# Local attention on Trainium2: the weighted sum of the three dilations moved from VectorE to GpSimd for three heads out of four

## Chip, cores and metric

One core of a Trainium2 (trn2) chip runs the whole program in one launch. The metric is the time of the program on the device in microseconds (us), the median of several runs. A profiled execution lists what each engine did: TensorE (PE in the profile; its weight loads are PEld), VectorE (DVE), ScalarE (ACT), GpSimd (POOL) and SyncE (SP), which here issues the DMAs.

## The reference

A trunk of two decoder layers over 1024 positions of width 1024, all in float32. The first layer mixes with gated DeltaNet heads and short convolutions, the second (odd) layer with four HGRN2 heads and four heads of dilated local attention; a SwiGLU network follows each. The change lies in the second layer's local attention. Every head attends three times, with dilations 1, 4 and 16, and the three outputs are added with weights that come from their log-sum-exps:

```python
for p, (window, dilation) in enumerate(SWA_PATTERNS):      # (128, 1), (512, 4), (2048, 16)
    o_p, lse_p = dilated_window_attention(sq[:, :, p], sk[:, :, p], sv[:, :, p], window, dilation)
    outs.append(o_p)
    lses.append(lse_p)
wts = jax.nn.softmax(jnp.stack(lses, axis=-1), axis=-1)
o_d = jnp.einsum('bthpd,bthp->bthd', jnp.stack(outs, axis=3), wts).reshape(b, t, SWA_HEADS * SWA_DH)
return jnp.concatenate([o_c.astype(h.dtype), o_d.astype(h.dtype)], axis=-1) @ w_out
```

## The kernel before

Most of the program is projections on TensorE: a float32 operand is split into a high part (ScalarE, line 103) and a remainder (VectorE, line 104), and three matmuls of 128x512 (lines 136 to 138) give one product. Weights come by DMA into two buffers `raw`.

`mixer_cd` is the second layer's mixer. Its Python code is a set of generators: `hg_chain` steps through HGRN2's eight units (four heads by two halves of 512 positions), `loc` through attention, and `tick`, called between pieces of the projections, advances them, so that their small matmuls stand between large ones in the order of the program. Within this mixer the engines' own orders are not written out by hand: a planner orders each engine's instructions at build time from the program's order, the dependences and its own estimates of durations. The order is fixed in the finished program, each engine runs its list in order, and an instruction whose input is late holds up what stands behind it on that engine.

Attention runs dilation 4 first, then 16, then 1 (`p` is 1, 2, 0). The outputs of the first two go to DRAM (`scr_o`) with their maxima and sums in two more columns. When a half (`g`) of a head (`h`) is done for dilation 1, `output` copies it from PSUM to SBUF (`ol`, line 2456) and starts `combine(h, g, ol, sums)`, eight in all. A combine

- loads the other two outputs into `cm0` and `cm1` (line 2482, two buffers each, so that a load must wait until the combine before the last has done with them);
- works out the three weights `w3` in a string of tiny VectorE instructions of 128x4 (lines 2488 to 2499, the first two of which read `cm0` and `cm1`);
- scales `cm0` and `cm1` on ScalarE (line 2503, eight of 128x128);
- multiplies `ol` by its weight (line 2504) and adds `cm0` and `cm1` to it (line 2506, two), each 128x512 and each dependent on the one before;
- two steps of `loc` later transposes `ol` on TensorE (line 2511), copies the result out of PSUM (line 2513) and stores it for the output projection (line 2514).

Beside it the HGRN2 units use VectorE (lines 2153 to 2161: differences and products of 128x256; 2173 to 2287 others), ScalarE, and for a few instructions GpSimd: a copy (2160), four copies of 32x128 into `attn` (2214) and a power of 128x4 (`rr`, line 2264), which VectorE's line 2266 waits for.

Of the kernel before, what the change touches and what calls it, by code (L numbers as in the profile page):

```python
# [16 lines left out]
MULT, ADD, SUB, MAX, MIN = ALU.mult, ALU.add, ALU.subtract, ALU.max, ALU.min  # L17

P = 128
# [37 lines left out]
def hybrid_trunk_kernel(ctx: ExitStack, tc: tile.TileContext, x_t, w_all, w_down, w_ba, vecs, c_f, c_i, c_rope, out):  # L57
    nc = tc.nc
    V, S, G, T = nc.vector, nc.scalar, nc.gpsimd, nc.tensor
# [34 lines left out]
    def psu():  # L94
        return ps.tile([P, HT], F32, tag="u", name="psu", bufs=3)
# [2002 lines left out]
    def mixer_cd(hn, hp, qkd, wv):  # L2098
# [5 lines left out]
        with ExitStack() as es:  # L2104
            def tl(tag, shape=(HT,), bufs=1):
                return wp.tile([P] + list(shape), F32, tag=tag, name=tag, bufs=bufs)
# [245 lines left out]
            class Attend:  # L2352
# [90 lines left out]
                def output(self, n):  # L2443
# [15 lines left out]
                    if p == 0:  # L2459
                        late.append(combine(h, g, ol, sums))  # L2460
                        next(late[-1])
                        return
# [14 lines left out]
            def combine(h, g, ol, sums):  # L2477

                t, st = [ol], [sums]
                for p in range(2):  # L2480
                    a = tl(f"cm{p}", (4, 132), 2)
                    dma(a[:, :, 0:P + 2],
                        scr_o[h, p, g * HT:(g + 1) * HT].rearrange("(j i) d -> i j d", i=P)[:, :, 0:P + 2])
                    t.append(a)
                    st.append(a[:, :, P:P + 2])
                yield
                mx, dn, w3, tmp = tl("mx", (4,)), tl("dn", (4,)), tl("w3", (3, 4)), tl("tmp4", (4,))
                V.tensor_tensor(mx, st[0][:, :, 0], st[1][:, :, 0], op=MIN)
                V.tensor_tensor(mx, mx, st[2][:, :, 0], op=MIN)
                for p in range(3):  # L2490
                    V.tensor_tensor(w3[:, p, :], st[p][:, :, 0], mx, op=SUB)
                S.activation(w3, w3, AF.Exp, scale=-1.0)
                for p in range(3):
                    d = dn if p == 0 else tmp
                    V.tensor_tensor(d, w3[:, p, :], st[p][:, :, 1], op=MULT)
                    if p:
                        V.tensor_tensor(dn, dn, tmp, op=ADD)
                V.reciprocal(tmp, dn)
                V.tensor_tensor(w3, w3, tmp[:, None, :].to_broadcast([P, 3, 4]), op=MULT)
                for p in range(1, 3):  # L2500
                    for j in range(4):
                        x, w = t[p][:, j, 0:P], w3[:, p, j:j + 1]
                        S.activation(x, x, AF.Copy, scale=w)  # L2503
                V.tensor_tensor(ol[:, :, 0:P], ol[:, :, 0:P], w3[:, 0, :, None].to_broadcast([P, 4, P]), op=MULT)
                for p in range(1, 3):
                    V.tensor_tensor(ol[:, :, 0:P], ol[:, :, 0:P], t[p][:, :, 0:P], op=ADD)  # L2506
                yield
                yield
                o = psu()
                for j in range(4):  # L2510
                    T.transpose(o[:, j * P:(j + 1) * P], t[0][:, j, 0:P], ident)
                go = tl("sw", bufs=2)
                S.copy(go, o)
                dma(catd[g][4 + h], go)
# [133 lines left out]
    E = mybir.EngineType  # L2648
# [205 lines left out]
```

## Time and profile before

| | |
|---|---|
| median of 3 runs | 2501.08 us (2499.98 to 2502.36) |
| profiled execution | 2501.29 us, of which 2499.5 us are the profile's span |
| TensorE matmul busy | 2482.9 us, 99% of the span |
| TensorE weight load busy | 2057.6 us, 82% |
| VectorE busy | 1693.6 us, 68% |
| ScalarE busy | 1101.1 us, 44% |
| GpSimd busy | 626.9 us, 25% |
| granted TensorE clock | 0.999 |
| the first and the last start of a line-2504 instruction | 1689.1 and 1766.4 us |
| line 2504 on VectorE | 8 instructions, median 692 ns |
| line 2506 on VectorE | 16 instructions, median 692 ns |

Busy time is the time in which an engine had an instruction in work; an instruction that waits inside for a shared resource counts as busy. Matmuls overlap, so TensorE's busy share says that it hardly ever stood, not that it worked at its peak. Times in the text are counted from the start of the span.

### The profile page before, as it was taken

The page shows a single profiled execution, that of the slowest core. Times are in us where ns is not written, and L with a number is a line of the kernel's source. Part 1 is how long each engine was busy: PE and PEld are TensorE (multiplying, and loading weights), DVE is VectorE, ACT ScalarE, POOL GpSimd, SP SyncE. Part 2 cuts the span into 40 slices and gives each one's busy share as a digit, 9 for nine tenths or more (in the row PEclk, how much of TensorE's full clock was granted, in tenths as well). Part 3 has the DMA queues.
Part 4 walks back from the last instruction along what each step waited for, and adds up shares of the span by engine and source line. Part 5 has one row for each costly group of instructions (what it writes and reads, how often), then busy time and mean ns, then how long its engine had stood idle before and what let it go on. Part 6 is the DMA issues. An engine that isn't in the chain of part 4 may idle for free. (4 is left out here: it accounts for less than half of the span.)

```text
span 2499.5 us, 37191 instructions
## 1 busy us (share of the span) xinstructions
PE 2482.9 (99%) x13715; PEld 2057.6 (82%) x13715; DVE 1693.6 (68%) x2811; ACT 1101.1 (44%) x1932; POOL 626.9 (25%) x591
## 2 busy tenths in 40 slices
PE   9999999999999999999999999999999999999998
PEld 7888888888888888888888888888888888888887
DVE  8987775686656665567798647788667555656654
ACT  5432134343333345344677435567534333334442
POOL 1321111323333300031466401100132333330001
PEclk9999999999999999999999999999999999999999
DMA  4535458236566688643344467875833555658753
GB/s 157 165 122 166 136 167 270 102 109 208 195 207 217 204 291 297 191 138 138 130 154 139 150 213 250 209 213 185 280 108 113 169 185 188 218 201 294 275 177 126
DMA packets 292975, 466.16 MB, mean 187 GB/s; under 512 B 49944, under 2 KB 146744, under 8 KB 292536
## 3 DMA queue, kind: packets, MB, share of 16 engines
q1 hardware_dynamic: 292504, 463.26, 56.2%
q8 instruction: 108, 1.77, 0.3%
q10 hardware_dynamic: 288, 0.52, 0.1%
q14 instruction: 75, 0.61, 0.1%
HBM read 314.18 MB, written 149.50 MB: 186 GB/s over the span
## 5 line engine op out<-in xcount | busy, mean ns | idle before, releaser
L104 DVE TENSOR_TENSOR w<-raw,w 128x1024 fp32r<-128x1024 f32 (+1 forms) x333 | 394.3, 1187 | 147.3 <-ACT w L103 146.8
L103 ACT CAST w<-raw 128x1024 fp32r<-128x1024 f32 (+1 forms) x333 | 315.2, 954 | 283.9 <-PE psu L138 126.5
L136 PE MATMUL psu<-hnh,w 128*128 128x512 f32 x772 | 308.7, 400 | 0.0
L138 PE MATMUL psu<-hnh,w 128*128 128x512 f32 x772 | 301.3, 390 | 0.0
L137 PE MATMUL psu<-hnl,w 128*128 128x512 f32 x772 | 301.1, 390 | 0.0
L199 POOL TENSOR_TENSOR acc<-acc,sq 128x512 f32<-128x512 f32 x52 | 78.2, 1504 | 442.8 <-ACT sq L195 398.6
L338 POOL TENSOR_TENSOR ws<-raw 128x512 f32<-128x512 f32 x54 | 70.5, 1305 | 433.8 <-DMA raw<-in_dram 224.5
L136 PEld LDWEIGHTS psu<-hnh,w 128*128 128x128 f32 x772 | 145.0, 188 | 31.0 <-ACT sq L195 0.8
L138 PEld LDWEIGHTS psu<-hnh,w 128*128 128x128 f32 x772 | 144.9, 188 | 31.0
L137 PEld LDWEIGHTS psu<-hnl,w 128*128 128x128 f32 x772 | 145.2, 188 | 28.0
L104 DVE TENSOR_TENSOR w<-ws,w 128x1024 fp32r<-128x1024 f32 x51 | 70.8, 1388 | 105.3 <-ACT w L103 105.2
L104 DVE TENSOR_TENSOR hidq<-hr,hidq 128x1024 fp32r<-128x1024 f32 x72 | 82.3, 1145 | 77.3 <-ACT hidq L103 76.9
L103 ACT CAST hidq<-hr 128x1024 fp32r<-128x1024 f32 x72 | 70.2, 979 | 102.3 <-DMA hr<-ts 60.1
L429 POOL TENSOR_TENSOR hid<-hid,c 128x512 f32<-128x512 f32 x44 | 63.1, 1433 | 171.8 <-ACT hid L428 171.6
L136 PE MATMUL psm<-hidq,w 128*128 128x512 f32 (+1 forms) x275 | 106.1, 386 | 0.0
L137 PE MATMUL psm<-hidq,w 128*128 128x512 f32 (+1 forms) x275 | 105.8, 385 | 0.0
L138 PE MATMUL psm<-hidq,w 128*128 128x512 f32 (+1 forms) x275 | 105.8, 385 | 0.0
L136 PE MATMUL psu<-t3h,w 128*128 128x512 f32 x240 | 93.4, 389 | 0.0
L137 PE MATMUL psu<-t3l,w 128*128 128x512 f32 x240 | 93.4, 389 | 0.0
L138 PE MATMUL psu<-t3h,w 128*128 128x512 f32 x240 | 93.4, 389 | 0.0
L136 PE MATMUL psu<-t4h,w 128*128 128x512 f32 x240 | 93.4, 389 | 0.0
L137 PE MATMUL psu<-t4l,w 128*128 128x512 f32 x240 | 93.4, 389 | 0.0
(616 smaller groups left out, 6617.1 us busy)
## 6 DMA issues: line engine op xcount, KB each, us to landing
raw<-in_dram SPq DMA_DIRECT2D x229, 512.0 KB, 4.4
sd<-in_dram SPq DMA_DIRECT2D x44, 512.0 KB, 4.0
hid<-hid SPq DMA_DIRECT2D x88, 256.0 KB, 3.2
sd<-sd SPq DMA_DIRECT2D x44, 512.0 KB, 3.0
hr<-ts SPq DMA_DIRECT2D x40, 512.0 KB, 4.7
raw<-sd SPq DMA_DIRECT2D x40, 512.0 KB, 4.6
qk<-z SPq DMA_DIRECT2D x52, 256.0 KB, 4.1
hd<-h SPq DMA_DIRECT2D x48, 256.0 KB, 3.4
```

What stands on the lines that cost most here:

```text
L103: S.copy(hi, src)
L104: eng.tensor_tensor(lo, src, hi.bitcast(F32), op=SUB)
L136: T.matmul(o, lh, rh, start=first and i == 0, stop=False, **kw)
L137: T.matmul(o, lh, rl, start=False, stop=False, **kw)
L138: T.matmul(o, ll, rh, start=False, stop=last and i == n - 1, **kw)
L199: (eng or G).tensor_tensor(a, a, q, op=ADD)
L338: G.tensor_tensor(s[:, HT:], b[:, :HT], b[:, HT:], op=ADD)
L429: G.tensor_tensor(h, h, self.c22.pop(f), op=MULT)
```

## The change

For heads 0, 1 and 2 the multiplication and the two additions of a combine are issued on GpSimd (`G`), for head 3 they stay on VectorE (`V`). Operands, shapes, dependences and the order of the program stay as they were; 18 of the 24 instructions change engine.

```diff
                         x, w = t[p][:, j, 0:P], w3[:, p, j:j + 1]
                         S.activation(x, x, AF.Copy, scale=w)
-                V.tensor_tensor(ol[:, :, 0:P], ol[:, :, 0:P], w3[:, 0, :, None].to_broadcast([P, 4, P]), op=MULT)
+                E = G if h < 3 else V
+                E.tensor_tensor(ol[:, :, 0:P], ol[:, :, 0:P], w3[:, 0, :, None].to_broadcast([P, 4, P]), op=MULT)
                 for p in range(1, 3):
-                    V.tensor_tensor(ol[:, :, 0:P], ol[:, :, 0:P], t[p][:, :, 0:P], op=ADD)
+                    E.tensor_tensor(ol[:, :, 0:P], ol[:, :, 0:P], t[p][:, :, 0:P], op=ADD)
                 yield
                 yield
                 o = psu()
```

## The prediction, made before the changed kernel was run

> **What bounds the kernel now.** I read the page's busy shares first, then the windows view of the stretch in which the eight combines run, then TensorE's waits there.
>
> ```profile
> span 2499.5 us, 37191 instructions
> ...
> PE 2482.9 (99%) x13715; PEld 2057.6 (82%) x13715; DVE 1693.6 (68%) x2811; ACT 1101.1 (44%) x1932; POOL 626.9 (25%) x591
> ```
> ```profile
> 1689.00:1772.00 83.00, 80.26 (x834) 68.47 (x821) 72.42 (x247) 64.34 (x183) 6.18 (x11) 1.00 0.63 198
> ```
> ```profile
> PE psg L2169 <- DVE m L2161: 0.9, 1, 0.9
> PE psg L2255 <- DVE st L2248: 0.7, 1, 0.7
> PE psu L2511 <- DVE ol L2506: 0.7, 1, 0.7
> PE psg L2196 <- DVE w L2491: 0.3, 1, 0.3
> ```
>
> TensorE bounds the whole: it stands idle for 2499.5 - 2482.9 = 16.6 us of the span. The windows row covers 83 us, from the first multiplication of a combine to the store of the last; its columns are the busy time (and count) of PE, PEld, DVE, ACT and POOL. VectorE is busy for 72.42 us here, 87% against 68% in the mean, so this is the stage in which taking work off it could count, and GpSimd with 6.18 us has room. But TensorE is busy for 80.26 us and lacks only 2.74 us, of which the waits view (total, times, longest) puts 2.6 us down to VectorE. That is the whole prize, and 0.7 us of it is not to be had: line 2511 there waited for the last combine, of head 3, which stays on VectorE. So at most 1.9 us can be gained in this stage. A difference under 0.2%, 5.0 us, is about what a measurement of this kernel can't tell from no change; I use that bound for the chances.
>
> **What is removed.** The groups of VectorE's instructions in the same stretch (columns: busy us, mean ns, then idle before):
>
> ```profile
> L2506 DVE TENSOR_TENSOR ol<-ol,cm 128x512 f32<-128x512 f32 x16 | 11.0, 688 | 4.7 <-ACT cm L2503 4.5
> ...
> L2504 DVE TENSOR_TENSOR ol<-ol,w 128x512 f32<-128x512 f32 x8 | 5.5, 690 | 2.5 <-ACT ol L2456 2.2
> L2287 DVE SCALAR_TENSOR_TENSOR xg<-xg,oc 128x512 f32<-128x512 f32 x7 | 5.0, 720 | 0.0
> L104 DVE TENSOR_TENSOR w<-raw,w 128x1024 fp32r<-128x1024 f32 x4 | 4.8, 1211 | 0.3 <-ACT w L103 0.3
> ...
> L104 DVE TENSOR_TENSOR hnl<-cin,hnh 128x512 fp32r<-128x512 f32 x7 | 4.8, 684 | 0.4 <-ACT hnh L103 0.4
> L2161 DVE TENSOR_TENSOR m<-m,q 128x256 f32<-128x256 f32 x7 | 3.0, 431 | 0.0
> ...
> L2153 DVE TENSOR_TENSOR m<-b 128x256 f32<-128x256 f32 x7 | 2.9, 415 | 0.0
> L2157 DVE TENSOR_TENSOR m<-m,kk 128x256 f32<-128x256 f32 x6 | 2.5, 418 | 0.0
> L2155 DVE TENSOR_TENSOR m<-b 128x256 f32<-128x256 f32 x6 | 2.5, 411 | 0.0
> L2497 DVE TENSOR_TENSOR dn<-dn,tmp 128x4 f32<-128x4 f32 x14 | 2.4, 170 | 0.1
> L2495 DVE TENSOR_TENSOR tmp<-w,cm 128x4 f32<-128x4 f32 x14 | 2.3, 162 | 0.0
> ```
>
> Six multiplications and twelve additions leave VectorE: 18 x 0.69 = 12.4 us. What is left there is 72.4 - 12.4 = 60.0 us.
>
> **What one of them costs on GpSimd.** No instruction of a combine has run there. The nearest rows are GpSimd's instructions of the same size with two inputs; line 1765 multiplies by a broadcast operand with four rows of 128, the closest in form (columns: min/median/max in ns).
>
> ```profile
> L1765 POOL TENSOR_TENSOR cx<-cx,masks x8: 1282/1414/2205, 87.9 to 225.2; 128x512 f32<-128x512 f32 x8
> ```
> ```profile
> L344 POOL TENSOR_TENSOR raw<-raw,ws x51: 1282/1294/2292, 539.1 to 2245.1; 128x512 f32<-128x512 f32 x51
> ```
>
> Both begin at 1.28 us and reach beyond 2.2. I take the median of the nearest form, 1.41 us; the ends for the range are 1.28 and 2.2.
>
> **Why the same instruction takes 1.28 or 2.2, and what that does to VectorE.** The timeline shows it. First a VectorE instruction with two inputs in SBUF beside a GpSimd one, then VectorE instructions that take their second tensor from PSUM (`psm`):
>
> ```profile
> 1057.93 2.31 DVE L104 TENSOR_TENSOR w<-raw,w 128x1024 fp32r<-128x1024 f32 x1
> ```
> ```profile
> 1057.75 1.41 POOL L199 TENSOR_TENSOR acc<-acc,sq 128x512 f32<-128x512 f32 x1 [6.19 <-ACT sq L195]
> ```
> ```profile
> 1100.69 2.06 DVE L261 SCALAR_TENSOR_TENSOR h<-h,vec,psm 128x512 f32<-128x512 f32 x3
> ```
> ```profile
> 1100.97 1.30 POOL L338 TENSOR_TENSOR ws<-raw 128x512 f32<-128x512 f32 x1 [4.22 <-DMA raw<-in_dram]
> ```
>
> Line 104's instruction of this form takes 1.21 us in the quoted group. Here it began 0.18 us after GpSimd's, took 2.31 us, and ended 1.08 us after GpSimd's had ended at 1059.16: it did its work after the other, not beside it. The three of line 261 took 0.69 us each beside GpSimd's 1.30, and neither shows a delay. So a GpSimd instruction can hold up a VectorE instruction whose two inputs are in SBUF for its whole length, and one with an input in PSUM not at all.
> The Trainium skill, "SBUF — State Buffer", section "Who interferes with whom", states it as a rule that speaks against this change: VectorE with two SBUF inputs and a GpSimd instruction that reads SBUF exclude each other, and whichever comes second waits until the first is finished. The rows at 1057.75 and 1057.93 agree.
>
> VectorE's instructions of the nine quoted groups from line 2287 on read two tensors in SBUF and sum to 30.2 us, half of the 60.0 us left. So I charge each moved instruction with half its length: 18 x 1.41 x 0.5 = 12.7 us of waiting put into VectorE's queue. The ends are 0 (the planner puts only PSUM work beside) and all, 18 x 1.41 = 25.4 us. At the middle value VectorE is relieved of nothing.
>
> **What waits for a longer chain.** The three instructions of a combine follow each other, 3 x 1.41 = 4.2 us. Before, with other VectorE work between them and waits for ScalarE's scaling, they took as long as this (first start and last, and TensorE's transposes behind them) in the combines that have the least time to spare, head 0's second and head 2's first:
>
> ```profile
> 1704.12 0.68 DVE L2504 TENSOR_TENSOR ol<-ol,w 128x512 f32<-128x512 f32 x1
> ...
> 1707.33 0.69 DVE L2506 TENSOR_TENSOR ol<-ol,cm 128x512 f32<-128x512 f32 x1 [0.31 <-ACT cm L2503]
> ...
> 1739.43 0.69 DVE L2504 TENSOR_TENSOR ol<-ol,w 128x512 f32<-128x512 f32 x1
> ...
> 1741.92 0.69 DVE L2506 TENSOR_TENSOR ol<-ol,cm 128x512 f32<-128x512 f32 x1
> ```
> ```profile
> 1699.64 0.60 PE L2511 MATMUL psu<-cf,ol 128*128 128x128 f32 x4
> ...
> 1709.76 0.60 PE L2511 MATMUL psu<-cf,ol 128*128 128x128 f32 x4
> ...
> 1743.45 0.60 PE L2511 MATMUL psu<-cf,ol 128*128 128x128 f32 x4
> ...
> 1755.98 0.60 PE L2511 MATMUL psu<-cf,ol 128*128 128x128 f32 x4
> ```
>
> Head 0's second: 1704.12 to 1708.02, 3.9 us, and 1.7 us to spare before the transposes at 1709.76; on GpSimd 0.3 us later, hidden. Head 2's first: 1739.43 to 1742.61, 3.2 us, and 0.8 us to spare; on GpSimd 1.0 us later, so TensorE waits 0.2 us (nothing at 1.28 us an instruction; at 2.2 the chain is 6.6 us and TensorE waits 2.6). The other four moved ones have more; the first and the last of them:
>
> ```profile
> 1691.28 0.68 DVE L2506 TENSOR_TENSOR ol<-ol,cm 128x512 f32<-128x512 f32 x1
> ...
> 1749.99 0.68 DVE L2506 TENSOR_TENSOR ol<-ol,cm 128x512 f32<-128x512 f32 x1
> ```
>
> They end 7.7 us before the transposes at 1699.64 and 5.3 us before those at 1755.98, so they cost nothing even at 2.2 us. On GpSimd's own queue the chain stands ahead of `rr`, of which VectorE's next step of HGRN2 waits; with 11 other instructions in 83 us they seldom meet, and I price that at nothing, at the high end at the one that would meet (`rr` at 1717.39, right behind head 1's first chain): 2 us on VectorE.
>
> **A wait that is added.** The loads of `cm0` and `cm1` for the combine after next wait on SP's queue until the additions have read the old contents, and VectorE waits for them at line 2489:
>
> ```profile
> 1706.71 1.71 SPq L2482 DMA_DIRECT2D cm<-scr_o  x2
> ...
> 1741.47 1.54 SPq L2482 DMA_DIRECT2D cm<-scr_o  x2
> ```
> ```profile
> 1711.94 0.17 DVE L2489 TENSOR_TENSOR mx<-mx,cm 128x4 f32<-128x4 f32 x1 [0.74 <-DMA cm<-scr_o]
> ...
> 1745.95 0.16 DVE L2489 TENSOR_TENSOR mx<-mx,cm 128x4 f32<-128x4 f32 x1
> ```
>
> At 1711.94 it already waited 0.74 us for the load that head 0's second combine had let go. The load behind head 2's first was issued by 1743.0, 3 us before its use at 1745.95, while the other took until 1711.94 from an issue by 1708.4, 3.5 us: it has nothing to spare either. So the two combines' lateness, 0.3 and 1.0 us, becomes 1.3 us of waiting at the head of VectorE's queue, with HGRN2's products (lines 2157, 2161) and the weights of the next combine behind it. At 2.2 us an instruction it would be 2.7 + 3.4 = 6.1 us. SP's later issues move back as much; none of the waits shown above is on a weight load, and I price that at nothing.
>
> **The sum.** VectorE: -12.4 + 12.7 + 1.3 = +1.6 us. Of its 83 - 72.4 = 10.6 us of slack, 2.6 us show up on TensorE, a quarter; a quarter of 1.6 is +0.4 us. TensorE waits 0.2 us more for head 2's transposes. The waits of 0.9 and 0.3 us at lines 2169 and 2196 come right after head 0's first combine has taken three instructions out of VectorE's time there; I give them half a chance to go, -0.6 us. Together 0.0 us: 2501.3 us for an execution like the profiled one, which is 0.2 us above the median, so **2501.1 us** as a median. Its own range is from the 1.9 us that can be gained to the 2.6 us that head 2's transposes lose at 2.2 us an instruction.
>
> **The rivals.**
> *GpSimd and VectorE take turns throughout, and it is slower.* Were every moved instruction to take 2.2 us because it waits for VectorE first, and VectorE to wait for it in full (25.4 us), VectorE would be late by 25.4 - 12.4 + 6.1 + 2 = 21.1 us. A quarter on TensorE is 5.3 us; head 2's transposes cost 2.6 us and head 0's second 1.0 us (2.7 later, 1.7 to spare). Sum +8.9 us: 2510 us. For it: half of VectorE's remaining work needs both inputs from SBUF, and the stage runs at 87%. Against: the two rows of GpSimd's instructions reach 2.2 us only at their maximum, with medians of 1.29 and 1.41. It decides from about 1.8 us an instruction.
> That is also what the skill's rule gives where all of VectorE's neighbours have two SBUF inputs; half of them have.
>
> *The relief arrives in full.* Only PSUM work stands beside GpSimd's, and all of TensorE's waits but head 3's go: -1.9 us, 2499.2 us. For it: 10.6 us of slack and a planner that knows the chain's length. Against: half of the neighbours can be blocked. It would still be within 0.2%.
>
> *The planner orders the rest of the mixer differently.* All engines' orders here follow its estimates. TensorE's loss to waits in this stage, 2.6 us in 83, is what one such order has; another may have none or twice that, 2498.5 to 2504 us. More than 5 us faster isn't in this stage at all (2.74 us idle); it would have to come from another order in a later stage.
>
> **How the numbers follow.** The forecast, 2501.1 with its own range of 2499.2 to 2503.7, has 0.70; the full relief 0.10; another order within 0.2% 0.05; the slower rival 0.12; something later that is faster by more than 0.2% 0.03. So faster 0.03, same 0.85, slower 0.12. The range, 2498.5 to 2506.5, takes in the relief and the other orders and ends halfway into the slower rival.
>
> **What would show it.** Lines 2504 and 2506 stand on POOL 18 times; at a mean of 1.3 to 1.5 us the price was right, from 1.8 the slower rival is at work. VectorE's group rows for lines 2153 to 2161, 2287 and 104 show means above 431, 720 and 1211 ns if it is blocked; if they stay, the relief is real. VectorE's wait for `cm<-scr_o` should grow from 0.74 to about 2 us. TensorE's idle time in the 83 us should stay at 2 to 4 us. The forecast is wrong if that passes 7 us, or if a later stage's TensorE time changes.

## The result and the profile after

The changed kernel takes 2507.72 us (median of 9 runs, 2505.88 to 2510.36) against 2501.01 us before (9 runs, 2499.93 to 2502.36): ratio 1.0027, 95% interval 1.0018 to 1.0036. It is 6.7 us slower, beyond the 0.2% bound, and above the range of 2498.5 to 2506.5. The forecast of no change was wrong; the rival that ends slower had the sign right, but by a mechanism that did not come (below).

The page of the kernel after (span, then busy us and counts), and the windows row of the same 83 us as before (PE, PEld, VectorE, ScalarE, GpSimd, granted clock):

```profile
span 2508.3 us, 37198 instructions
...
PE 2488.1 (99%) x13715; PEld 2061.7 (82%) x13715; DVE 1689.0 (67%) x2793; ACT 1101.7 (44%) x1932; POOL 653.2 (26%) x609
```
```profile
1689.00:1772.00 83.00, 77.41 (x851) 65.68 (x850) 62.29 (x214) 59.16 (x172) 28.45 (x29) 0.96 0.56 176
```

VectorE's busy time fell from 72.42 to 62.29 us, as the change says (the work in the window is by then some us late). But TensorE's idle time rose from 2.74 to 5.59 us, and the granted clock fell from 1.00 to 0.96, which the prediction had nowhere. TensorE's waits after (total, times, longest):

```profile
PE psg L2169 <- DVE m L2161: 1.6, 1, 1.6
PE psg L2196 <- DVE dn L2497: 1.6, 1, 1.6
PE psu L2512 <- DVE ol L2507: 0.9, 1, 0.9
```

Line 2512 is the old 2511, still only head 3's combine. The waits at lines 2169 and 2196, to which the prediction gave half a chance to go, grew from 0.88 and 0.33 us to 1.65 and 1.59 us. To see where the loss lies, I lined up the projections' matmuls (lines 136 to 138), which come in all but the same order in these kernels (at least 9677 of 9681), and took how late each is against the profiled execution before. The lag is already 1.69 us at 1688 us, ahead of the first combine, so that much is not the change's. From there it grows to 8.90 us at 1800 and stays: +0.5 us at 1690 (a wait for a DMA, line 2378), **+4.8 us between 1694 and 1701**, +1.9 us between 1732 and 1775. The 4.8 us stand right behind the first combine, of head 0. VectorE and GpSimd there, after:

```profile
1691.93 0.16 DVE L2491 TENSOR_TENSOR w<-stat,mx 128x4 f32<-128x4 f32 x1 [2.97 <-POOL ol L2505]
1692.01 1.33 DVE L2491 TENSOR_TENSOR w<-cm,mx 128x4 f32<-128x4 f32 x2
1693.27 0.68 DVE L2287 SCALAR_TENSOR_TENSOR xg<-xg,oc 128x512 f32<-128x512 f32 x1
1693.87 1.51 DVE L2153 TENSOR_TENSOR m<-b 128x256 f32<-128x256 f32 x1
1695.30 0.63 DVE L2155 TENSOR_TENSOR m<-b 128x256 f32<-128x256 f32 x1
```
```profile
1690.86 1.04 POOL L2505 TENSOR_TENSOR ol<-ol,w 128x512 f32<-128x512 f32 x1 [10.78 <-ACT ol L2456]
1691.97 3.12 POOL L2507 TENSOR_TENSOR ol<-ol,cm 128x512 f32<-128x512 f32 x2
```

Two things are new. First, the weights of the next combine (line 2491) wait 2.97 us, until GpSimd's multiplication has read `w3`, of which there is one buffer. Second, beside GpSimd's two additions (1691.97 to 1695.09) line 2153 takes 1.51 us instead of 0.41, and even the 128x4 instructions of line 2491 take 1.33 us for two instead of 0.23 (as noread2 has them, below). In the kernel before, VectorE had waited 1.84 us for ScalarE's `ol` just ahead of this place and then did the combine itself. Less the 2.2 us by which TensorE is late here already, line 2153 after begins at 1691.7, only 0.4 us earlier than before, although three instructions of 0.69 us were taken off:

```profile
1689.10 0.69 DVE L2504 TENSOR_TENSOR ol<-ol,w 128x512 f32<-128x512 f32 x1 [1.84 <-ACT ol L2456]
...
1692.09 0.41 DVE L2153 TENSOR_TENSOR m<-b 128x256 f32<-128x256 f32 x1
```

TensorE behind it, after and then before:

```profile
1696.72 0.46 PE L2169 MATMUL psg<-e 128*32 128x32 f32 x32
1698.83 0.46 PE L2169 MATMUL psg<-m 128*32 128x32 f32 x32 [1.65 <-DVE m L2161]
1700.88 0.45 PE L2196 MATMUL psg<-m 128*32 128x32 f32 x16 [1.59 <-DVE dn L2497]
1701.25 0.70 PE L2201 MATMUL psg<-e 128*64 128x64 f32 x8
1701.88 2.08 PE L2378 MATMUL psm<-k,q 128*128 128x256 f32 x4
```
```profile
1695.87 0.46 PE L2169 MATMUL psg<-m 128*32 128x32 f32 x32 [0.88 <-DVE m L2161]
1696.26 1.13 PE L2378 MATMUL psm<-k,q 128*128 128x256 f32 x4
1697.72 0.33 PE L2196 MATMUL psg<-m 128*32 128x32 f32 x16 [0.33 <-DVE w L2491]
```

Lines 2169 and 2196 read `m`, which VectorE's lines 2157 and 2161 finish; the rows name what VectorE had ended last. The waits here are 1.65 + 1.59 = 3.24 us against 0.88 + 0.33 = 1.21, so 2.0 us longer. And the four matmuls of line 2378 took 2.08 us instead of 1.13. Three windows of 3.41 us in a row, after, show why (behind the window's length TensorE's busy time; the third number from the end is the granted clock):

```profile
1697.02:1700.43 3.41, 0.62 (x53) 0.42 (x39) 3.40 (x12) 1.73 (x6) 0.00 (x0) 1.00 0.37 103
1700.43:1703.84 3.41, 2.96 (x29) 2.34 (x30) 2.52 (x8) 1.28 (x3) 0.00 (x0) 0.50 0.00 0
1703.84:1707.26 3.42, 3.42 (x17) 3.42 (x16) 3.27 (x16) 2.57 (x11) 1.88 (x4) 0.50 0.00 0
```

TensorE was busy for 0.62 of 3.41 us, and then the clock was halved for 6.83 us. What is left of the 4.8 us, 2.8, I put down to the clock; line 2378 alone has 0.95 us of it. The Trainium skill, "TensorE: Matmul & The Clock Gate", Part 1, has the clock halved after an idle window of 3.4 us and given back after a busy one. The length agrees; but here two waits, neither above 1.65 us, with small matmuls between them, were enough.

### The profile page after: what moved, and what is told of

The parts are those of the page before. It is cut to its first block, busy times and chain, and to the rows that moved or that the text cites. A ratio compares the mean times of both kernels' runs of the same rounds, so it can differ in the third digit from the quotient of the medians.

```text
span 2508.3 us, 37198 instructions
## 1 busy us (share of the span) xinstructions
PE 2488.1 (99%) x13715; PEld 2061.7 (82%) x13715; DVE 1689.0 (67%) x2793; ACT 1101.7 (44%) x1932; POOL 653.2 (26%) x609
```

## The experiments

Four theories for the 4.8 us, with the letters that the expectations use: the wait for the single buffer of `w3` (A); GpSimd's reads holding up VectorE's instructions with two inputs in SBUF (B, "the port"); the halved clock that follows from either (C); and the planner's new order, bad in itself (D). Lags below are taken as above, each from 1692 to 1701 us of the kernel before. Ratios are against the kernel before on the same chip, with 95% intervals.

### Two buffers for the weights (w3two)

```diff
-tl("w3", (3, 4))
+tl("w3", (3, 4), 2)
```

> The changed kernel with two buffers for the weights w3 in place of one. Theory A (the weights' buffer): VectorE's first write of the next combine's weights (line 2491) waited 2.97 us for GpSimd's multiplication, which still had to read the old ones; with a second buffer that wait goes, TensorE's waits at lines 2169 and 2196 (1.65 and 1.59 us) fall to the 0.9 and 0.3 us of before, the clock stays at 1.00, and the time is 2501 to 2503 us. Theory B (the shared port): the wait goes but GpSimd's additions still hold up VectorE's instructions with two inputs in SBUF, and the time stays at 2505 to 2508 us.

2508.05 us, 1.0024 (1.0014 to 1.0034): no gain. VectorE at the place, with GpSimd's additions from 1690.16 to 1693.34:

```profile
1690.08 0.69 DVE L2287 SCALAR_TENSOR_TENSOR xg<-xg,oc 128x512 f32<-128x512 f32 x1 [2.58 <-ACT xg L2286]
1690.69 1.50 DVE L2153 TENSOR_TENSOR m<-b 128x256 f32<-128x256 f32 x1
1692.12 1.52 DVE L2155 TENSOR_TENSOR m<-b 128x256 f32<-128x256 f32 x1
```

Line 2491's wait is gone, but VectorE then waits for ScalarE at line 2287 instead, and lines 2153 and 2155 are both held. The lag is +4.8 us again. The buffer is a real wait and not the cause. (VectorE's own order changed a little with it; noread2 below settles the same in the order of the kernel after.)

### Only the additions on GpSimd (adds)

```diff
-E.tensor_tensor(ol[:, :, 0:P], ol[:, :, 0:P], w3[:, 0, :, None]..., op=MULT)
+V.tensor_tensor(ol[:, :, 0:P], ol[:, :, 0:P], w3[:, 0, :, None]..., op=MULT)
```

> The changed kernel with the multiplication back on VectorE, for heads 0 to 2 the two additions alone on GpSimd. GpSimd then reads no weights. Theory A: no wait of line 2491 for GpSimd, no drop of the clock, 2501 to 2503 us. Theory B: 12 of the 18 instructions are still on GpSimd and their port with them, so two thirds of the loss stay: 2504.5 to 2507 us.

2508.09 us, 1.0027 (1.0017 to 1.0038): the additions alone cost all of it. Lag +4.9 us. One tiny instruction of VectorE beside GpSimd's first addition, at 1689.56:

```profile
1689.59 1.28 DVE L2491 TENSOR_TENSOR w<-stat,mx 128x4 f32<-128x4 f32 x1
```

It takes 1.28 us, as long as an addition on GpSimd, where it takes 0.16 by itself.

### The first combine only, and all but the first (first, notfirst)

```diff
-E = G if h < 3 else V
+E = G if (h, g) == (0, 0) else V                  # first
+E = G if h < 3 and (h, g) != (0, 0) else V        # notfirst
```

> Only the first combine (head 0, first half) on GpSimd, the other seven on VectorE. Theory A, and the lag between the two traces, put 5.3 of the 7.2 us at this one combine: line 2491 waits about 3 us for GpSimd, the clock drops behind it, and the time is 2505 to 2507 us. If the loss is spread over all six combines, as a port shared throughout would have it, a sixth of it is left: 2501 to 2503 us.

> The changed kernel with the first combine (head 0, first half) back on VectorE, the other five of heads 0 to 2 on GpSimd. In the trace of the changed kernel 4.9 of 7.2 us of the lag came at the first combine and 1.9 us at the later ones (1732 to 1770 us): 2502.5 to 2504 us. If the loss goes wherever GpSimd is first used: 2506 to 2508 us.

first: 2503.96 us, 1.0010 (1.0002 to 1.0019); notfirst: 2503.82 us, 1.0009 (1.0000 to 1.0017). The trace of first has the whole lag of 4.9 us at the place, and gives 1.3 back up to 1770 us, where VectorE does the combines. notfirst has none there (+0.05) and +2.9 between 1708 and 1775, of which 2.6 between 1732 and 1748. So the loss has two parts. In the trace the first combine holds the larger; in the times the two can't be told apart, and first came out under the 2505 to 2507 us that theory A gave it.

All but the first with two buffers for `w3` (wnotfirst):

> As the run that leaves out the first combine, with two buffers for w3: the version that keeps as much of the change as may pay. Theories A and B: without the wait for the weights the later combines cost less, 2500 to 2502.5 us; if the port alone is what costs there, 2502.5 to 2504 us as with one buffer.

2504.11 us, 1.0011 (1.0003 to 1.0020): the second buffer doesn't help the later combines either.

### GpSimd writes and reads nothing (noread2)

All 18 instructions on GpSimd become pairs of memsets of `ol`; the outputs of heads 0 to 2 aren't combined. The order of instructions on TensorE, VectorE and ScalarE is that of the kernel after, and GpSimd's chain at the first combine is nearly as long (six memsets from 1688.11 to 1691.80, 3.7 us, against 4.2).

```diff
-E.tensor_tensor(ol[:, :, 0:P], ...)
+[G.memset(ol[:, :, 0:P], 0.0) for _ in range(2)] if h < 3 else E.tensor_tensor(ol[:, :, 0:P], ...)
```

> The changed kernel in which each of GpSimd's 18 multiplications and additions is replaced by two memsets of the same tile (0.53 us each): the three outputs of heads 0 to 2 are not added, zeros are stored. TensorE's, VectorE's and ScalarE's orders are those of the changed kernel to the instruction; GpSimd writes, but reads nothing, neither the weights nor cm. Theory B (the port, with A's wait beside it): VectorE's instructions keep their lengths, the clock stays at 1.00 behind the first combine, 2499.5 to 2502 us. Theory D (the new order is bad in itself): TensorE's waits and the clock's drop stay, 2506 to 2508 us.

2498.76 us, 0.9988 (0.9979 to 0.9997): 9 us below the kernel after and below the kernel before. Its windows row, TensorE's waits and VectorE's instructions at the place:

```profile
1687.00:1768.00 81.00, 79.17 (x883) 68.56 (x882) 60.65 (x228) 64.66 (x185) 24.31 (x47) 1.00 0.66 205
```
```profile
PE psu L2512 <- DVE ol L2507: 0.9, 1, 0.9
PE psg L2196 <- DVE dn L2497: 0.6, 1, 0.6
PE psg L2169 <- issue: 0.4, 1, 0.4
```
```profile
1688.69 0.16 DVE L2491 TENSOR_TENSOR w<-stat,mx 128x4 f32<-128x4 f32 x1 [2.44 <-ACT cm L2503]
...
1689.78 0.42 DVE L2153 TENSOR_TENSOR m<-b 128x256 f32<-128x256 f32 x1
1690.11 0.42 DVE L2155 TENSOR_TENSOR m<-b 128x256 f32<-128x256 f32 x1
```

The order is therefore not bad in itself: D falls. With writing alone on GpSimd the two instructions take 0.42 us and the clock stays at 1.00. The memsets also read neither `w3` nor `cm`, so waits for these tiles go too. At the first combine that isn't what counts: VectorE still waits 2.44 us at line 2491, now for ScalarE, where it waited 2.97 us for GpSimd, and TensorE's two waits are 1.0 us in sum all the same. What is gone is the lengthening of the instructions behind it. The Trainium skill, "SBUF — State Buffer", "Who interferes with whom", says that a GpSimd instruction that only writes SBUF does not contend with VectorE's second input; this run agrees.

### Reads added to the kernel before (ghost, ghostset)

The kernel before, with nothing moved, and two additions on GpSimd into a tile that nobody reads (ghost), or five memsets of it (ghostset), issued at the first combine. The orders of TensorE, VectorE and ScalarE are those of the kernel before.

```diff
+gs = tl("gs", (4, P)); cz = t[2][:, :, 0:P]
+(h, g) == (0, 0) and [G.tensor_tensor(gs, cz, cz, op=ADD) for _ in range(2)]     # ghost
+(h, g) == (0, 0) and [G.memset(gs, 0.0) for _ in range(5)]                       # ghostset
```

> The kernel before, all three instructions of every combine on VectorE, plus two GpSimd additions of 128x512 in head 0's first combine that read cm1 (once ScalarE has scaled it) and write a tile that nobody reads; the orders of TensorE, VectorE and ScalarE are those of before. Nothing is moved and nobody waits for the two. Theory B (the port): they hold up VectorE's instructions with two SBUF inputs for about 1.1 us each, TensorE's waits at lines 2169 and 2196 grow from 1.2 to 2.5 us or more, and with the clock's drop behind it (theory C) the time is 2504 to 2507 us. If instead it is the planner's new order that costs the time, as theory D has it, this one stays at 2500 to 2502 us.

> The same with five memsets on GpSimd in place of the two additions: about the same time on GpSimd (0.53 us each), but they read nothing. Theory B in the form that only GpSimd's reading excludes VectorE's second input: no effect, 2500 to 2502 us. If any GpSimd work at that place does it: as the one with the additions.

ghost: 2503.53 us, 1.0006 (0.9997 to 1.0015), by the time alone not told from no change, and under the 2504 to 2507 us expected. The mean granted clock of each execution tells them apart: 0.998 in 10 of 11, against 0.999 in all 33 of the kernel before on that chip. Its trace shows the thing itself; GpSimd's two additions, then VectorE:

```profile
1691.93 2.49 POOL L2504 TENSOR_TENSOR gs<-cm 128x512 f32<-128x512 f32 x2 [11.38 <-ACT cm L2503]
```
```profile
1692.01 1.50 DVE L2506 TENSOR_TENSOR ol<-ol,cm 128x512 f32<-128x512 f32 x1
1693.44 1.52 DVE L2287 SCALAR_TENSOR_TENSOR xg<-xg,oc 128x512 f32<-128x512 f32 x1
1694.88 0.90 DVE L2506 TENSOR_TENSOR ol<-ol,cm 128x512 f32<-128x512 f32 x1
```

Beside the two reads on GpSimd these three take 3.92 us in sum; in the kernel before they take 0.69, 0.93 and 0.68, 2.30 us. TensorE's wait at line 2169 became 1.78 us, the clock was halved for 3.41 us, and the lag is +2.0 us. ghostset, 2500.68 us, 0.9997 (0.9989 to 1.0006), missed as a test: the memsets depended on nothing and ran earlier, none of them beside these instructions. It only shows that five more instructions on GpSimd cost nothing.

### Work added to VectorE instead (vdelay3)

```diff
+(h, g) == (0, 0) and [V.tensor_tensor(gs, cz, cz, op=ADD) for _ in range(3)]
```

> The kernel before with three more VectorE additions of 128x512 (0.69 us each, 2.1 us) in head 0's first combine, into a tile that nobody reads; GpSimd isn't used. Theory C (the clock follows from TensorE's idle time, whatever delays VectorE): VectorE is as late as behind GpSimd's instructions, the clock drops for 3.4 to 6.8 us, 2503 to 2506 us. If the drop needs GpSimd: no drop, and at most the 2.1 us, 2501 to 2503.5 us.

> The kernel before with three more VectorE additions in head 0's first combine once more, for its trace. Its time was that of the kernel before, so theory C expects that TensorE's idle time at 1694 to 1701 us did not grow (1.2 us as before) and the clock stayed at 1.00. If the idle time grew to 3 us and the clock stayed at 1.00 all the same, the drop is not tied to the idle time alone.

2501.85 us, 1.0000 (0.9991 to 1.0009), with 3 x 0.69 = 2.1 us more for VectorE at the same place. The profiled execution of vdelay3 took 6460 us and tells nothing of this, so the trace is that of vdelay3b, the same kernel in a single execution of 2504.75 us (the kernel before on that chip: 2499.64 to 2505.72). TensorE there:

```profile
1696.24 0.46 PE L2169 MATMUL psg<-e 128*32 128x32 f32 x32
1696.63 1.13 PE L2378 MATMUL psm<-k,q 128*128 128x256 f32 x4
1697.60 0.27 PE L2430 MATMUL psm<-cf,sc 128*128 128x128 f32 x1
1699.26 0.46 PE L2169 MATMUL psg<-m 128*32 128x32 f32 x32 [1.39 <-DVE m L2161]
```

The planner, which knows how long VectorE's own instructions take, put line 2378 into the gap that in the kernel before stood ahead of the second group of line 2169. The lag is +0.4 us and the clock stays at 1.00. Since TensorE's order changed, this does not test whether the same delay without GpSimd would halve the clock; the 2503 to 2506 us expected for that did not come. A delay that the planner can see is filled; one by contention, of which its estimates hold nothing, is not. That the estimates lack it is my reading of these two orders; it was not tried by changing them.

### Matmuls in the gap (fill, firstfill3, addsfill3)

To keep TensorE busy in the wait at line 2169, extra matmuls of 128x384 whose result nobody uses, five on the kernel after (fill), three on first and on adds.

```diff
+[T.matmul(od[:, P:4 * P], kk[:, 0:P], q[:, P:4 * P], start=True, stop=True) for n in range(5) if (h, half, i) == (3, 0, 1)]
 blocks(od[:, i * P:(i + 1) * P], ms[i], ms[i])
```

> The changed kernel with five more matmuls of 128x384 (into a part of the PSUM tile that is written again later) where TensorE waited 1.65 us at line 2169 in the first half of head 3's HGRN2 unit; about 1.6 us of work. Theory C (the clock): the granted clock fell to 0.5 for 6.8 us because TensorE had been nearly idle for some 3.4 us; kept busy, it stays at 1.00 there, and although TensorE has more to do the time falls by 2 to 4 us, to 2503.5 to 2506 us. If the drop of the clock comes from something else, or is not what costs the time, it stays at 2507 to 2510 us.

> The kernel with only the first combine on GpSimd, plus three matmuls of 128x384 (0.7 us each) where TensorE waited 2.11 us at line 2169. Theory C: TensorE is not idle enough for the clock to fall, the granted clock stays 1.00 through 1690 to 1710 us, and the lag behind the kernel before at that place is about 2 us in place of 4.8: 2500.5 to 2502.5 us in all. If the drop isn't what costs the time: 2503.5 to 2505 us.

> The kernel with the additions alone on GpSimd, plus three matmuls of 128x384 (0.7 us each) where TensorE waited 1.82 us at line 2169. Theory C: the clock stays at 1.00 there and the lag at 1701 us is about 2.3 us in place of 4.9; the whole, if the later part stays the same, 2505 to 2506 us in place of 2508.1. If the clock drops all the same: 2508 us or more.

fill: 2518.97 us, 1.0071 (1.0058 to 1.0084), a miss: the order of the later combines changed with it, and VectorE's wait for `w3` became the main one (columns: total, times, longest):

```profile
DVE w L2491 <- POOL ol L2505: 17.6, 5, 5.8
```

At the place itself its lag was +2.4 us with the clock at 1.00. firstfill3: 2504.67 us, 1.0011 (1.0002 to 1.0019); addsfill3: 2507.31 us, 1.0024 (1.0015 to 1.0033). firstfill3 at the place:

```profile
1693.98 2.20 PE L2191 MATMUL psg<-q,kk 128*128 128x384 f32 x6
1696.12 0.46 PE L2169 MATMUL psg<-m 128*32 128x32 f32 x32
1697.72 0.33 PE L2196 MATMUL psg<-m 128*32 128x32 f32 x16 [1.15 <-DVE dn L2497]
```

With 2.1 us of useless matmuls the lag at the place fell from 4.9 to 1.9 us (first) and from 4.9 to 2.1 us (adds): work in place of the wait, and no halved clock. That is in line with 2 to 3 us for the clock at the place (in first, the waits less those of before leave 2.4). In the time of the whole hardly anything is left of it (ratios 1.0011 against 1.0010 and 1.0024 against 1.0027), and both times missed what was expected if the clock counted in full, 2500.5 to 2502.5 and 2505 to 2506 us. The traces lose time again later, where VectorE's order is a different one: addsfill3 +3.9 us between 1701 and 1775 against 2.1 in adds.

The mean granted clock on record for every execution says how often it falls. first has 0.997 in 8 of 11 and 0.998 in the rest, firstfill3 0.999 in 8 and 0.998 in 3; the kernel before, beside first, 0.999 in all 22. So the drop is the rule, and the extra matmuls mostly prevent it. Of after and w3two, the nine executions with 0.997 have a median of 2508.3 us, the three with 0.999 took 2505.7, 2505.9 and 2507.1. These few put the clock at about 2 us of the whole and leave over 4 us of the loss without it.

### The kernel before with two buffers for the weights (bw3two)

> The kernel before with two buffers for the weights w3: a control for the other runs with two. All theories: 2500 to 2502.5 us; VectorE's and ScalarE's orders change a little, so a deviation tells what another order alone does.

2500.00 us, 0.9994 (0.9985 to 1.0003): not told from the kernel before. No version that computes the whole was clearly faster than before.

## Why the prediction was wrong, step by step

**The price on GpSimd** was right, even high. Predicted 1.41 us an instruction (1.28 to 2.2):

```profile
L2505 POOL TENSOR_TENSOR ol<-ol,w x6: 1040/1042/1362, 1690.9 to 1755.4; 128x512 f32<-128x512 f32 x6
```
```profile
L2507 POOL TENSOR_TENSOR ol<-ol,cm x12: 1273/1287/1773, 1692.0 to 1757.9; 128x512 f32<-128x512 f32 x12
```

The medians are 1.04 and 1.29 us, the mean of all 18 is 1.27; the multiplication lies below the lower bound. The rival "take turns" was to decide from 1.8 us an instruction, and it came out slower at 1.3. That it had the sign was luck: it charged VectorE 25.4 us of waiting, and VectorE had 6.9. What counted was not the mean but where a blocked instruction stands.

**The exclusion** was found, but its charge was a mean: half of 25.4 us, 12.7 us. Each instruction of VectorE in the 83 us held against the median of its line and shape in the same trace, they were 6.9 us longer in sum, against 0.3 us in the kernel before. Seven instructions have 6.5 of the 6.9 us; the group of line 2153, 415 ns in the kernel before, and that of line 2491, 167 ns with no idle time:

```profile
L2153 DVE TENSOR_TENSOR m<-b 128x256 f32<-128x256 f32 x7 | 4.0, 571 | 0.0
...
L2491 DVE TENSOR_TENSOR w<-stat,mx 128x4 f32<-128x4 f32 x7 | 2.2, 316 | 7.4 <-ACT cm L2503 4.4 <-POOL ol L2505 3.0
```

**The step that failed** is the charge to TensorE, "a quarter of 1.6 is +0.4 us" with "half a chance" that the waits at 2169 and 2196 go, -0.6 us. The quarter is an average over the stage. With what was measured in place of the estimates, -12.4 + 6.9 held + 3.0 for `w3` + 1.2 for `cm` = -1.3 us for VectorE, it would even have given a gain of 0.3 us. The half chance took it that VectorE's time is freed where the instructions stood. The 1.84 us wait for `ol` in the kernel before says that VectorE had a hole ahead of this combine: GpSimd's start is bound by the same copy, so taking three instructions off VectorE freed little there (in noread2, where nothing is held, the two waits fell by only 0.2 us), and the two additions then held lines 2491, 2153 and 2155, ahead of what TensorE's next two waits hang on. Measured: +2.0 us of waits where -0.6 had been put.

**The clock** was missing as a term: 2.8 us at the place by this trace, about 2 us by the times of executions with it and without. The granted clock of 1.00 in the stage was quoted and not asked how long it would last.

**The wait for `w3`** was missing too: VectorE's wait of 2.97 us for GpSimd's multiplication. By w3two it cost nothing here, since VectorE waits for ScalarE next; in fill it reached 17.6 us.

**The loads of `cm`** were right: predicted "from 0.74 to about 2 us".

```profile
DVE mx L2489 <- DMA cm<-scr_o: 1.9, 1, 1.9
```

**Head 2's transposes**, predicted 0.2 us late: TensorE has no wait there. **What would show it** worked in part: line 2153 passed its 431 ns bound with 571 and line 2155 with 464, while 2157, 2161 (417 and 415) and 104 (1211) did not and 2287 hardly did (725); and TensorE's idle time of 5.59 us passed the 2 to 4 us forecast. It didn't reach the limit of 7 us, since a halved clock makes busy time, not idle time.

**The relief in full** (2499.2 us) is what noread2 comes near with 2498.76: in a kernel that leaves the sums of heads 0 to 2 out, VectorE's time is worth 2 to 3 us, if GpSimd reads nothing.

**Open**: the 1.9 us between 1732 and 1775. notfirst shows them without the first combine, and wnotfirst that a second buffer of `w3` doesn't take them away. There too instructions of lines 2153 and 2155 were held beside GpSimd's additions (1.53 and 1.49 us at 1730.17 and 1731.63), the wait for `cm` grew, and the order is new; these were not told apart.

## What to carry to other kernels

Ask of work moved to GpSimd not how long it takes there but which VectorE instructions with two SBUF inputs the planner will set beside it, and what waits for these; a stage's mean hides the one place where it counts. Look whether VectorE was waiting anyway where the moved work stood: then little is freed. Where TensorE has small matmuls and two short waits close together, half a microsecond more can halve its clock for microseconds (next section), so count that as a term of its own.

## What the hardware showed beyond that

- The clock halved without TensorE standing still. The window of 3.41 us ahead of a drop was busy for 0.62 us (after) and 1.63 us in ghost, whose two windows around the drop are below. The emptiest stretch of that length at this place was busy for 2.20 us in the kernel before (from 1694.32) and 2.00 us in vdelay3b (from 1697.70), and there the clock stayed at 1.00. The drop ended after a window that was busy throughout, 3.40 us in ghost, and went on after one of 2.96 us (the second of the three rows of after):

```profile
1696.69:1700.10 3.41, 1.63 (x69) 1.11 (x67) 3.38 (x14) 1.68 (x6) 0.00 (x0) 1.00 0.52 158
...
1700.10:1703.50 3.40, 3.40 (x35) 2.39 (x31) 3.28 (x12) 2.87 (x8) 0.00 (x0) 0.50 0.01 2
```

- Exclusion hits tiny instructions too: 128x4 took 1.28 us in adds instead of 0.16.
- On GpSimd the multiplication by `w3`, whose values are repeated along the last axis, takes 1.04 us and the addition of two whole tiles 1.29 us (medians); on VectorE both take 0.69 us. Multiplication as such isn't shorter: line 1765, from which the price was taken, multiplies by a tile that is repeated over the four rows of 128, and takes at least 1.28 us. Why, no run here shows.
